# S5 mixer: the back rotation's two products go unsummed into the output products, the S5 matrices come on GpSimd's DMA queue, an input weight is split later

## The chip, the cores and the metric

The kernel runs on one core of a Trainium2 chip. The metric is the device time of one execution, in microseconds (us). Before the change it is 1264.65 us, the median of three runs (1264.57 to 1264.82). Five engines run their own instruction streams and meet at semaphores: TensorE (PE in the profile; its weight loads are PEld), VectorE (DVE), ScalarE (ACT), GpSimd (POOL) and SyncE (SP), which here only issues DMAs.

## The reference

The model is a trunk of four residual layers over 256 tokens of width 1024. The mixers are HGRN2, mLSTM, S5 and HGRN2 again, each followed by a SwiGLU layer. The change lies in the S5 mixer, a complex diagonal state space with 64 groups of 16 channels and 64 states each:

```python
def _s5_mixer(x, w_in, a_re, a_im, log_dt, b_re, b_im, c_re, c_im, d_skip, w_out):
    u = (x @ w_in)
    ...                      # abar, bbar from a, dt, b
    def step(carry, ub):
        bu_re = jnp.einsum('blgc,gpc->blgp', ub, bbar_re)
        bu_im = jnp.einsum('blgc,gpc->blgp', ub, bbar_im)
        pr, pi, sr, si = lax.associative_scan(_s5_combine, (a_r, a_i, bu_re, bu_im), axis=1)
        ...
        y = jnp.einsum('blgp,gcp->blgc', sr, c_re) - jnp.einsum('blgp,gcp->blgc', si, c_im)
    ...
    y = jax.nn.gelu(y + d_skip * u)
    za, zb = jnp.split(y @ w_out, 2, axis=-1)
    return za * jax.nn.sigmoid(zb)
```

## The kernel before

Large products are made of three: each fp32 weight is split into a high half (`hi`, a copy on ScalarE, line 129) and a low half (`lo`, a subtraction on VectorE, line 130), and `mm3` issues hi times hi, lo times hi and hi times lo. Weights arrive in units of 1 MB (tile `w`, line 108, issued by SP); `wstage` takes the next unit of a fixed plan and stages up to `ahead` units further.

The S5 stage works on four pairs of blocks, p = 0 to 3, each with 16 of the 64 groups; the 256 tokens are cut into 64 chunks of four, and the scans run over the chunks. For each pair `load_in` brings the input matrices (tiles `bm`, twice 512 KB) and the rotation tables (`cs`, 768 KB), `load_out` the output matrices (`ch`, 512 KB, and `cw`, twice 256 KB). Then:

- `inputs(p)` multiplies the transposed input projection `s5u` by `bm` on TensorE (line 1151).
- `forth(p)` rotates the result on VectorE (four products, one sum) and runs four scans (line 1167), so that a real scan does for the complex one.
- `back(p)` rotates back: two products (lines 1173 and 1174) and their sum (line 1176), which goes to `s5hs`.
- `outputs(p)` adds on TensorE, in two PSUM banks of the tag `t`, the products with `cw` (line 1190) and the C products of `ch` with `s5hs` (line 1197); ScalarE applies gelu into `ys`.
- `turn` transposes `ys` on TensorE (line 1207) into another `t` bank, copies the high half (ScalarE) and subtracts for the low half (VectorE, line 1212), into `xx`. The output products `a` (`out_piece`, weights `w_so`) of that pair start behind it, and the bank is free again.

`land` transposes the input projection into `s5u` on VectorE (line 1128); `project` makes that projection. `table_out` writes the tables `cs` to memory in an earlier step, during the layer before. The program is written as a list of such calls; a scheduler sets the order on each engine from it, by priorities and costs of its own, and puts in the waits. In `s5hs` the scanned states are shifted by one position, so that a C product takes the state ahead of its chunk; what happens inside a chunk comes from the `cw` products.

Of the kernel before, what the change touches and what calls it, by code (L numbers as in the profile page):

```python
# [9 lines left out]
F32 = mybir.dt.float32  # L10
# [4 lines left out]
ALU = mybir.AluOpType  # L15
AX = mybir.AxisListType

P = 128
# [16 lines left out]
class Trunk:  # L35
# [821 lines left out]
    def s5_prepare(self):  # L857


        nc, a = self.nc, self.a  # L860
# [4 lines left out]
        c = self.s5const  # L865
# [6 lines left out]
        tt, ts, stt = nc.vector.tensor_tensor, nc.vector.tensor_scalar, nc.vector.scalar_tensor_tensor  # L872
# [11 lines left out]
        def temps(*shape):  # L884
            n = int(np.prod(shape))
            dims = "abcd"[: len(shape)]
            out = []
            for tag, bufs in (("t0", 1), ("t1", 1)):
                t = tile_(tag, [P, 1024], bufs=bufs)[:, :n]
                kw = dict(zip(dims, shape))  # L890
                out.append(t.rearrange(f"p ({' '.join(dims)}) -> p {' '.join(dims)}", **kw))
            return out
# [84 lines left out]

        def table_out(b):
            cs, neg = k["cs"], temps(16, 64)[0]
            nc.scalar.mul(neg, cs[:, 1], -1.0)  # L980
            for i in range(2):
                for row, x in enumerate((cs[:, 0], neg, cs[:, 1])):
                    nc.sync.dma_start(self.s5_cs[2 * b + i][:, :, row].rearrange("p e (f c) -> p e f c", f=4),
                                      x[:, 8 * i : 8 * i + 8].rearrange("p (e f) c -> p e f c", e=2))
# [82 lines left out]
        for b in range(2):  # L1067
            spans[b] += [lambda b=b: table_start(b)] + [lambda n=n: table_double(n) for n in (1, 2, 4, 8, 16, 32)] + [lambda b=b: table_out(b)]
# [8 lines left out]
    def s5(self, gb):  # L1077
        nc, tc = self.nc, self.tc
        tt = nc.vector.tensor_tensor
# [15 lines left out]
        with tc.tile_pool(name=self.uid("s5"), bufs=1, reuse_waits="tile") as mp, \  # L1095
# [1 line left out]
            tl = lambda tag, shape, bufs=2: wp.tile(shape, F32, tag=tag, name=self.uid(tag), bufs=bufs)  # L1097
            u = mp.tile([P, 32, 64], F32, name="s5u")
            rr = [mp.tile([P, 2, 4, 64], F32, name=f"s5rr{i}") for i in range(2)]
            hs = [mp.tile([P, 2, 2, 4, 65], F32, name=f"s5hs{i}") for i in range(2)]  # L1100
            rot = [mp.tile([P, 2, 2, 256], F32, name=f"s5rot{i}") for i in range(3)]
            for r in rr:
                nc.gpsimd.memset(r[:, :, :, 0:1], 0.0)
            for h in hs:
                nc.gpsimd.memset(h[:, :, :, :, 0:1], 0.0)
            bm, cw, ch, tables, wi, pxs = {}, {}, {}, {}, {}, {}

            def load(dst, tag, src, i, bufs=2):
                dst[i] = tl(tag, list(src[i].shape), bufs)
                nc.sync.dma_start(dst[i], src[i])  # L1110

            def load_in(p):
                for b in (2 * p, 2 * p + 1):
                    load(bm, "bm", self.s5_b, b)
                load(tables, "cs", self.s5_cs, p)

            def load_out(p):
                load(ch, "ch", self.s5_ch, p)
                for b in (2 * p, 2 * p + 1):
                    load(cw, "cw", self.s5_cw, b, 4)  # L1120

            load_in(0)
            load_out(0)

# [4 lines left out]

            def project(n, h, tag, mid=None):  # L1130
                if n not in wi:
                    wi[n] = self.wstage("w_si", 2 * n) + self.wstage("w_si", 2 * n + 1, ahead=1 - n)
                ps = self.bank(tag)
                self.as_part({h: ps}, wi[n], mid=mid)
                return ps
# [17 lines left out]

            def forth(p):

                x, g, y = rot
                r, cs = rr[p % 2], tables[p]
                r4 = self.s5_r4[:, 8 * p : 8 * p + 8].rearrange("p (e f) -> p e f", e=2)
                nc.scalar.copy(r[:, :, :, 1:], r4[:, :, :, None].broadcast_to([P, 2, 4, 63]))
                for e in range(2):  # L1160
                    px = pxs.pop(2 * p + e).rearrange("p (r x) -> p r x", r=2)
                    tt(x[:, e], px, cs[:, e, 0:1].broadcast_to([P, 2, 256]), ALU.mult)
                    tt(y[:, e], px[:, ::-1], cs[:, e, 1:3], ALU.mult)
                tt(x, x, y, ALU.add)
                for e in range(2):
                    for i in range(2):
                        nc.vector.tensor_tensor_scan(g[:, e, i], r[:, e].rearrange("p f c -> p (f c)"), x[:, e, i], 0.0, ALU.mult, ALU.add)  # L1167

            def back(p):

                x, g, y = rot
                h, cs = hs[p % 2], tables[p]
                tt(x, g, cs[:, :, 0:1].broadcast_to([P, 2, 2, 256]), ALU.mult)
                tt(y, g[:, :, ::-1], cs[:, :, 2:0:-1], ALU.mult)
                many = lambda t: t.rearrange("p e r (f c) -> p (e r f) c", f=4)
                tt(h.rearrange("p e r f c -> p (e r f) c")[:, :, 1:], many(x), many(y), ALU.add)

            pieces, todo = [], []
            col = lambda f: slice(f * P, (f + 1) * P)
# [1 line left out]
            def outputs(p):  # L1181


                py, h = [self.bank("t") for _ in range(2)], hs[p % 2]
                at = lambda g, e, f: py[g][64 * e : 64 * e + 64, 64 * f : 64 * f + 64].rearrange("p (j c) -> p j c", j=4)
                for f in range(4):
                    for g in range(2):
                        for e in range(2):
                            w = cw[2 * p + e].rearrange("p (f j g c) -> p f j g c", f=4, j=4, g=2)
                            nc.tensor.matmul(at(g, e, f), u[:, 8 * p + 4 * e + f, :], w[:, f, :, g, :], start=f == 0, stop=False, skip_group_check=True)  # L1190
                for f in range(4):
                    for i in range(2):
                        for g in range(2):
                            for e in range(2):
                                r = slice(64 * g, 64 * g + 64)
                                c = ch[p].rearrange("p i j (f c) -> p i j f c", f=8)
                                nc.tensor.matmul(at(g, e, f), h[r, e, i, f, 0:64], c[r, i, :, 4 * e + f, :], start=False, stop=f == 3 and i == 1, skip_group_check=True)
                ys = tl("ys", [P, 4, P], 1)
                for g in range(2):
                    self.act(ys.rearrange("p j (f g c) -> p g f j c", f=4, g=2)[:, g], py[g][:, 0:256].rearrange("p (f j c) -> p f j c", f=4, j=4), AF.Gelu_apprx_tanh)  # L1200
                todo.append((ys, 2 * p))
# [13 lines left out]
            def few(n):  # L1215
                for _ in range(min(n, len(pieces))):
                    out_piece(0, *pieces.pop(0))

            land(project(0, 0, "g"), 0, 0)
            land(project_part(1, 0, "g"), 0, 1)  # L1220
            self.table("gelu_apprx_tanh_and_others")
            inputs(0)
            last = project_part(1, 1, "a")
            forth(0)
            land(last, 8, 1)
            load_in(1)
            more = project(1, 0, "a")
            back(0)
            inputs(1)
            outputs(0)  # L1230
            forth(1)
            load_out(1)
            land(more, 16, 0)
            more = project(1, 1, "a", lambda: turn(*todo.pop(0)))
            land(more, 16, 1)
            back(1)
            load_in(2)
            inputs(2)
            outputs(1)
            forth(2)  # L1240
            load_out(2)
            few(3)
            turn(*todo.pop(0))
            few(1)
            back(2)
            load_in(3)
            inputs(3)
            outputs(2)
            forth(3)
            load_out(3)  # L1250
# [194 lines left out]
```

## Time and profile before

| | us |
|---|---|
| median of three runs | 1264.65 |
| profiled execution, its time | 1264.65 |
| profiled execution, its span | 1262.9 |
| TensorE busy | 1241.5 |
| VectorE busy | 957.0 |
| ScalarE busy | 706.3 |
| GpSimd busy | 36.1 |

The S5 stage lies between about 641 and 736 us of the span. The granted TensorE clock is full there. In the profile's rows an instruction is named by line, engine, operation and tiles, the output ahead of the arrow; a bracket gives the idle time of the engine ahead of a row and what ended it. Small fp32 products appear as two records each.

### The profile page before, as it was taken

The numbers are of one execution on the slowest core, as the hardware profiler recorded it, in microseconds if no ns is written. First come the engines' busy times: TensorE is split into PE (matmuls) and PEld (weight loads), VectorE is DVE, ScalarE is ACT, GpSimd is POOL, SyncE is SP. The second block draws the span as 40 slices with busy tenths as digits, with TensorE's granted clock in tenths as the row PEclk, the third lists the DMA queues.
The fourth block names the chain that finished last, engine by engine and source line by source line (L and its number), as shares of the span: only waits on it lengthen the run. The fifth ranks groups of instructions, "written<-read, shape, count | busy, mean of one in ns | idle before, by whom it ended". The sixth has DMA issues, their size and how long they took to land. (4 is left out here: it accounts for less than half of the span.)

```text
span 1262.9 us, 21506 instructions
## 1 busy us (share of the span) xinstructions
PE 1241.5 (98%) x8541; PEld 1037.0 (82%) x8541; DVE 957.0 (76%) x1703; ACT 706.3 (56%) x1144; POOL 36.1 (3%) x58
## 2 busy tenths in 40 slices
PE   9999999999999999999998999999999999999997
PEld 7977888888798888888876678888879778888886
DVE  6887899876787799866599687666595887766664
ACT  7755576565467555666443455555458654555551
POOL 0000000000100100000000000000000000000000
PEclk9999999999999999999999999999999999999999
DMA  8733466765373266656569446555545432745530
GB/s 317 292 135 134 173 220 229 254 221 200 108 277 142 100 256 238 231 202 231 176 244 350 175 162 249 190 200 177 190 179 192 159 132 106 276 172 195 189 144 34
DMA packets 46340, 247.91 MB, mean 196 GB/s; under 512 B 5504, under 2 KB 11024, under 8 KB 19872
## 3 DMA queue, kind: packets, MB, share of 16 engines
q1 hardware_dynamic: 46112, 246.46, 53.4%
q8 instruction: 67, 1.10, 0.3%
q14 instruction: 33, 0.27, 0.1%
q0 software_dynamic: 128, 0.09, 0.0%
HBM read 233.94 MB, written 12.58 MB: 195 GB/s over the span
## 5 line engine op out<-in xcount | busy, mean ns | idle before, releaser
L130 DVE TENSOR_TENSOR lo<-w,hi 128x1024 fp32r<-128x1024 f32 x389 | 471.8, 1219 | 115.7 <-ACT hi L129 107.9
L129 ACT CAST hi<-w 128x1024 fp32r<-128x1024 f32 x389 | 407.2, 1051 | 198.8 <-PE a L160 118.1
L189 PE MATMUL g<-xx,hi 128*128 128x512 f32 x1024 | 358.2, 395 | 0.0
L192 PE MATMUL g<-xx,lo 128*128 128x256 f32 x1024 | 267.1, 281 | 0.0
L189 PEld LDWEIGHTS g<-xx,hi 128*128 128x128 f32 x1024 | 186.7, 188 | 34.6
L192 PEld LDWEIGHTS g<-xx,lo 128*128 128x128 f32 x1024 | 192.5, 188 | 10.3
L159 PE MATMUL g<-hi,xx 128*128 128x512 f32 (+1 forms) x416 | 167.7, 404 | 3.1 <-ACT xx L269 2.9
L161 PE MATMUL g<-lo,xx 128*128 128x512 f32 (+1 forms) x416 | 165.7, 400 | 0.1
L160 PE MATMUL g<-hi,xx 128*128 128x512 f32 (+1 forms) x416 | 164.7, 397 | 0.0
L160 PE MATMUL a<-hi,hl 128*128 128x512 f32 x344 | 135.4, 394 | 0.0
L159 PE MATMUL a<-hi,hh 128*128 128x512 f32 x344 | 135.4, 396 | 0.0
L161 PE MATMUL a<-lo,hh 128*128 128x512 f32 x344 | 135.4, 394 | 0.0
L329 ACT COPY sum<-g 128x256 f32<-128x256 f32 x128 | 47.7, 373 | 147.7 <-PE g L189 147.6
L330 DVE TENSOR_TENSOR sum<-g,sum 128x256 f32<-128x256 f32 x128 | 54.1, 423 | 69.4 <-ACT sum L329 68.8
L159 PEld LDWEIGHTS g<-hi,xx 128*128 128x128 f32 x416 | 78.4, 189 | 21.9 <-ACT xx L269 4.7
L161 PEld LDWEIGHTS g<-lo,xx 128*128 128x128 f32 x416 | 78.2, 188 | 18.4 <-DVE lo L130 1.5
L160 PEld LDWEIGHTS g<-hi,xx 128*128 128x128 f32 x416 | 78.5, 189 | 15.9
L161 PEld LDWEIGHTS a<-lo,hh 128*128 128x128 f32 x344 | 64.6, 188 | 15.0
L160 PEld LDWEIGHTS a<-hi,hl 128*128 128x128 f32 x344 | 64.5, 188 | 15.0 <-DVE hl L319 0.5
L159 PEld LDWEIGHTS a<-hi,hh 128*128 128x128 f32 x344 | 64.1, 188 | 13.5 <-ACT hh L318 0.6
L159 PE MATMUL g<-xx,hi 128*128 128x256 f32 x200 | 56.6, 283 | 0.0
L160 PE MATMUL g<-xx,lo 128*128 128x256 f32 x200 | 56.5, 283 | 0.0
(299 smaller groups left out, 1729.1 us busy)
## 6 DMA issues: line engine op xcount, KB each, us to landing
w<-in_w_gu SPq DMA_DIRECT2D x88, 1024.0 KB, 4.8
w<-in_w_dn SPq DMA_DIRECT2D x44, 1024.0 KB, 4.8
w<-in_w_hg SPq DMA_DIRECT2D x30, 1024.0 KB, 4.9
w<-in_w_ml SPq DMA_DIRECT2D x12, 1024.0 KB, 5.1
gb<-in_ln SPq DMA_DIRECT2D x8, 1024.0 KB, 4.6
w<-in_w_ho SPq DMA_DIRECT2D x8, 1024.0 KB, 4.9
w<-in_w_so SPq DMA_DIRECT2D x8, 1024.0 KB, 8.8
s5b<-st SPq DMA_DIRECT2D x16, 256.0 KB, 2.0
```

The lines of the kernel that those rows point to most:

```text
L129: self.nc.scalar.copy(hi, x)
L130: self.nc.vector.tensor_tensor(lo, x, hi.bitcast(F32), ALU.subtract)
L159: mm(ps, lh, rh, start=start, stop=False)
L160: mm(ps, ll, rh, start=False, stop=False)
L161: mm(ps, lh, rl, start=False, stop=stop)
L189: whole = lambda: mm(ps, hi[:, c], self.xx[:, k].rearrange("p i t -> p (i t)"), start=k == 0, stop=k == KD - 1)
L192: mm(ps[:, S:], lo[:, c], self.xh[:, k], start=False, stop=False)
L329: nc.scalar.copy(t, ps[:, S:])
L330: nc.vector.tensor_tensor(t, ps[:, 0:S], t, ALU.add)
```

## The change

`back` no longer sums. It writes its two products to two tiles, `hs[0]` and `hs[1]`, shifted by one element, and the C products run over both: 64 instead of 32 for a pair. For that, one column of the tables is set to zero when they are made. There were two `hs` tiles, one for each second pair; now the two belong to one pair, so that the next `back` waits for this pair's C products. Scratch tiles `rot` go from three to two. The loads of `bm`, `cs`, `ch` and `cw` are issued by GpSimd instead of SP, and `bm` has four buffers instead of two. In `project`, the second input weight unit no longer stages a third one with it.

```diff
@@ table_out
             cs, neg = k["cs"], temps(16, 64)[0]
+            nc.gpsimd.memset(cs[:, :, :, 63:64], 0.0)
@@ s5
-            hs = [mp.tile([P, 2, 2, 4, 65], F32, name=f"s5hs{i}") for i in range(2)]
-            rot = [mp.tile([P, 2, 2, 256], F32, name=f"s5rot{i}") for i in range(3)]
+            hs = [mp.tile([P, 1025], F32, name=f"s5hs{i}") for i in range(2)]
+            rot = [mp.tile([P, 2, 2, 256], F32, name=f"s5rot{i}") for i in range(2)]
...
-                nc.sync.dma_start(dst[i], src[i])
+                nc.gpsimd.dma_start(dst[i], src[i])
...
-                    load(bm, "bm", self.s5_b, b)
+                    load(bm, "bm", self.s5_b, b, 4)
@@ project
-                    wi[n] = self.wstage("w_si", 2 * n) + self.wstage("w_si", 2 * n + 1, ahead=1 - n)
+                    wi[n] = self.wstage("w_si", 2 * n) + self.wstage("w_si", 2 * n + 1, ahead=0)
@@ back
-                x, g, y = rot
-                h, cs = hs[p % 2], tables[p]
-                tt(x, g, cs[:, :, 0:1].broadcast_to([P, 2, 2, 256]), ALU.mult)
-                tt(y, g[:, :, ::-1], cs[:, :, 2:0:-1], ALU.mult)
-                many = lambda t: t.rearrange("p e r (f c) -> p (e r f) c", f=4)
-                tt(h.rearrange("p e r f c -> p (e r f) c")[:, :, 1:], many(x), many(y), ALU.add)
+                g, cs = rot[1], tables[p]
+                for h, src, w in zip(hs, (g, g[:, :, ::-1]), (cs[:, :, 0:1].broadcast_to([P, 2, 2, 256]), cs[:, :, 2:0:-1])):
+                    tt(h[:, 1:].rearrange("p (e r x) -> p e r x", e=2, r=2), src, w, ALU.mult)
@@ outputs
-                    for i in range(2):
+                    for i, h in ((0, hs[0]), (1, hs[0]), (0, hs[1]), (1, hs[1])):
...
-                                nc.tensor.matmul(at(g, e, f), h[r, e, i, f, 0:64], c[r, i, :, 4 * e + f, :], ...)
+                                x = 64 * (8 * e + 4 * i + f)
+                                nc.tensor.matmul(at(g, e, f), h[r, x : x + 64], c[r, i, :, 4 * e + f, :], ...)
```

The scheduler orders the changed program anew. (In these rows a scan is named by its general form, and numbers behind a name count the tiles.) On VectorE, around the second pair's back rotation and the first turn's subtraction (`xx` from `t1273`), before:

```order
L1167 SCALAR_TENSOR_TENSOR s5rot1_6918<-s5rr1_6914,s5rot0_6917 128x256 x4
L1212 TENSOR_TENSOR xx_83<-t1273_7304,xx_83 128x4x2x64
L1173 TENSOR_TENSOR s5rot0_6917<-s5rot1_6918,cs1257_7115 128x1024
L1128 STREAM_TRANSPOSE s5u_6912<-a1272_7291 128x16x32
L1174 TENSOR_TENSOR s5rot2_6919<-s5rot1_6918,cs1257_7115 128x1024
L130 TENSOR_TENSOR lo1301_7507<-w1299_7504,hi1300_7506 128x1024
L1176 TENSOR_TENSOR s5hs1_6916<-s5rot0_6917,s5rot2_6919 128x16x64
L130 TENSOR_TENSOR lo1303_7511<-w1299_7504,hi1302_7510 128x1024
```

and of the change:

```order
L1168 SCALAR_TENSOR_TENSOR s5rot1_6920<-s5rr1_6916,s5rot0_6919 128x256 x4
L1175 TENSOR_TENSOR s5hs0_6917<-s5rot1_6920,cs1252_7106 128x1024
L1175 TENSOR_TENSOR s5hs1_6918<-s5rot1_6920,cs1252_7106 128x1024
L130 TENSOR_TENSOR lo1301_7570<-w1299_7567,hi1300_7569 128x1024
L1212 TENSOR_TENSOR xx_83<-t1273_7336,xx_83 128x4x2x64
L130 TENSOR_TENSOR lo1303_7574<-w1299_7567,hi1302_7573 128x1024
L130 TENSOR_TENSOR lo1319_7807<-w1317_7804,hi1318_7806 128x1024
L1129 STREAM_TRANSPOSE s5u_6914<-a1272_7323 128x16x32
L130 TENSOR_TENSOR lo1321_7811<-w1317_7804,hi1320_7810 128x1024
```

The turn's subtraction stood ahead of the back rotation and now stands behind its two products and a split; the transposition into `s5u`, for which the third pair's `inputs` wait, stands behind the subtraction and two further splits. At the fourth pair and the third turn (`t1316`), VectorE before:

```order
L1167 SCALAR_TENSOR_TENSOR s5rot1_6918<-s5rr1_6914,s5rot0_6917 128x256 x4
L1212 TENSOR_TENSOR xx_83<-t1316_7695,xx_83 128x4x2x64
L1173 TENSOR_TENSOR s5rot0_6917<-s5rot1_6918,cs1307_7540 128x1024
L1174 TENSOR_TENSOR s5rot2_6919<-s5rot1_6918,cs1307_7540 128x1024
L130 TENSOR_TENSOR lo1334_7813<-w1332_7810,hi1333_7812 128x1024
L1176 TENSOR_TENSOR s5hs1_6916<-s5rot0_6917,s5rot2_6919 128x16x64
```

and of the change:

```order
L1168 SCALAR_TENSOR_TENSOR s5rot1_6920<-s5rr1_6916,s5rot0_6919 128x256 x4
L1175 TENSOR_TENSOR s5hs0_6917<-s5rot1_6920,cs1307_7602 128x1024
L1175 TENSOR_TENSOR s5hs1_6918<-s5rot1_6920,cs1307_7602 128x1024
L130 TENSOR_TENSOR lo1334_7938<-w1332_7935,hi1333_7937 128x1024
L1212 TENSOR_TENSOR xx_83<-t1316_7789,xx_83 128x4x2x64
```

Here too the subtraction went behind two products and a split. On TensorE the fourth pair's first eight cw products (16 records) stood ahead of the first output product that waits for that subtraction (line 160 into `a1285`, behind three that do not); now all its cw and C products stand behind such products. GpSimd's queue of the change, from the normalisation's power of the first half (`rs1223`) to the third pair's tables (`cs1276`) (a part is left out, with loads of the same kinds):

```order
L202 TENSOR_TENSOR rs1223_6840<-rs1223_6840,root_79 128x1
L1111 DMA bm1234_6925<-s5b0_1809 128x1024
L1111 DMA bm1235_6927<-s5b1_1810 128x1024
L1111 DMA cs1236_6929<-s5cs0_1833 128x1536
L202 TENSOR_TENSOR rs1229_6877<-rs1229_6877,root_79 128x1
L1111 DMA ch1237_6931<-s5ch0_1825 128x1024
...
L1111 DMA bm1274_7358<-s5b4_1813 128x1024
L1111 DMA bm1275_7360<-s5b5_1814 128x1024
L1111 DMA bm1305_7598<-s5b6_1815 128x1024
L1111 DMA bm1306_7600<-s5b7_1816 128x1024
L1111 DMA cs1276_7362<-s5cs2_1835 128x1536
```

Before, GpSimd had only the two powers and small clears here. The fourth pair's `bm` now stand ahead of the third pair's `cs`, and two `bm` and a `cs` ahead of the second power (`rs1229`).

More of the change, by code (lines that the diff above doesn't have):

```diff
@@ L1104, in s5 @@
             for h in hs:
-                nc.gpsimd.memset(h[:, :, :, :, 0:1], 0.0)
+                nc.gpsimd.memset(h[:, 0:1], 0.0)
             bm, cw, ch, tables, wi, pxs = {}, {}, {}, {}, {}, {}
@@ L1154, in forth @@
             def forth(p):
-                x, g, y = rot
+                x, g = rot
                 r, cs = rr[p % 2], tables[p]
@@ L1162, in forth @@
                     tt(x[:, e], px, cs[:, e, 0:1].broadcast_to([P, 2, 256]), ALU.mult)
-                    tt(y[:, e], px[:, ::-1], cs[:, e, 1:3], ALU.mult)
-                tt(x, x, y, ALU.add)
+                    tt(g[:, e], px[:, ::-1], cs[:, e, 1:3], ALU.mult)
+                tt(x, x, g, ALU.add)
                 for e in range(2):
@@ L1169, in back @@
             def back(p):
-                x, g, y = rot
-                h, cs = hs[p % 2], tables[p]
-                tt(x, g, cs[:, :, 0:1].broadcast_to([P, 2, 2, 256]), ALU.mult)
-                tt(y, g[:, :, ::-1], cs[:, :, 2:0:-1], ALU.mult)
-                many = lambda t: t.rearrange("p e r (f c) -> p (e r f) c", f=4)
-                tt(h.rearrange("p e r f c -> p (e r f) c")[:, :, 1:], many(x), many(y), ALU.add)
+                g, cs = rot[1], tables[p]
+                for h, src, w in zip(hs, (g, g[:, :, ::-1]), (cs[:, :, 0:1].broadcast_to([P, 2, 2, 256]), cs[:, :, 2:0:-1])):
+                    tt(h[:, 1:].rearrange("p (e r x) -> p e r x", e=2, r=2), src, w, ALU.mult)
             pieces, todo = [], []
@@ L1181, in outputs @@
             def outputs(p):
-                py, h = [self.bank("t") for _ in range(2)], hs[p % 2]
+                py = [self.bank("t") for _ in range(2)]
                 at = lambda g, e, f: py[g][64 * e : 64 * e + 64, 64 * f : 64 * f + 64].rearrange("p (j c) -> p j c", j=4)
@@ L1196, in outputs @@
                                 c = ch[p].rearrange("p i j (f c) -> p i j f c", f=8)
-                                nc.tensor.matmul(at(g, e, f), h[r, e, i, f, 0:64], c[r, i, :, 4 * e + f, :], start=False, stop=f == 3 and i == 1, skip_group_check=True)
+                                x = 64 * (8 * e + 4 * i + f)
+                                nc.tensor.matmul(at(g, e, f), h[r, x : x + 64], c[r, i, :, 4 * e + f, :], start=False, stop=f == 3 and i == 1 and h is hs[1], skip_group_check=True)
                 ys = tl("ys", [P, 4, P], 1)
```

## Prediction

> **What bounds the kernel now.** I read the page first, then the windows of the stage that the change touches, then the chain of waits there, then TensorE's and VectorE's timelines. On the page, TensorE is the busy engine and carries the largest share of the chain; the third row prices a weight's copy on ScalarE (busy us, mean ns):
>
> ```profile
> PE 1241.5 (98%) x8541; PEld 1037.0 (82%) x8541; DVE 957.0 (76%) x1703; ACT 706.3 (56%) x1144; POOL 36.1 (3%) x58
> PE 41%; DVE 3%; ACT 1%; issue 0%; DVEq 0%; POOL 0%; ACTq 0%; POOLq 0%
> L129 ACT CAST hi<-w 128x1024 fp32r<-128x1024 f32 x389 | 407.2, 1051 | 198.8 <-PE a L160 118.1
> ```
>
> That average hides the S5 stage. The table of windows (us; busy time with instruction counts of PE, PEld, DVE, ACT, POOL; granted clock; DMA share; GB/s) shows the opposite there:
>
> ```profile
> 657.00:668.00 11.00, 9.34 (x237) 7.79 (x227) 10.93 (x15) 0.71 (x2) 0.00 (x0) 1.00 0.87 320
> 668.00:683.00 15.00, 12.65 (x291) 10.13 (x288) 14.91 (x19) 8.28 (x10) 0.00 (x0) 1.00 0.81 304
> 683.00:697.00 14.00, 11.61 (x278) 9.43 (x282) 13.88 (x17) 3.76 (x5) 0.00 (x0) 1.00 0.97 384
> 697.00:711.00 14.00, 12.53 (x136) 9.30 (x131) 14.00 (x17) 4.91 (x6) 0.00 (x0) 1.00 0.44 171
> 711.00:736.00 25.00, 24.62 (x165) 19.39 (x162) 12.77 (x17) 10.67 (x13) 0.00 (x0) 1.00 0.36 126
> ```
>
> From 657 to 711 VectorE never rests and TensorE does; after 711 TensorE is full again. The DMA engines are 97% busy from 683 to 697. The chain of waits says the same in order of time (start, duration, what): VectorE up to the third turn's subtraction (L1212), then TensorE without a break to the last turn's transposes (L1207).
>
> ```profile
> 683.85 0.68 DVE s5rot L1162
> ...
> 704.87 0.96 DVE xx L1212
> ...
> 718.70 0.45 PE t L1207 x4
> ...
> 720.29 1.08 DVE xx L1212
> ```
>
> TensorE's timeline names each rest and its releaser in brackets (records here come in twos: 64 records of L1197 are the 32 products of a pair):
>
> ```profile
> 667.36 0.47 PE L1151 MATMUL g<-s5u,bm 128*32 128x64 f32 x17 [1.66 <-issue]
> 668.84 1.16 PE L1197 MATMUL t<-ch,s5hs 64*64 64x64 f32 x64
> 669.93 0.50 PE L159 MATMUL a<-hi,xx 128*128 128x512 f32 x1
> 670.27 0.39 PE L160 MATMUL a<-hi,xx 128*128 128x512 f32 x1
> 670.50 0.39 PE L161 MATMUL a<-lo,xx 128*128 128x512 f32 x1
> 677.73 1.03 PE L1190 MATMUL t<-cw,s5u 128*64 128x64 f32 x28 [1.24 <-DVE xx L1212]
> 679.48 1.99 PE L1151 MATMUL g<-s5u,bm 128*32 128x64 f32 x128 [0.29 <-DVE s5u L1128]
> 682.95 1.16 PE L1197 MATMUL t<-ch,s5hs 64*64 64x64 f32 x64 [0.82 <-DVE s5hs L1176]
> 693.08 1.03 PE L1190 MATMUL t<-cw,s5u 128*64 128x64 f32 x28 [1.26 <-DVE xx L1212]
> 696.60 1.16 PE L1197 MATMUL t<-ch,s5hs 64*64 64x64 f32 x64 [1.13 <-DVE s5hs L1176]
> 703.28 0.69 PE L1190 MATMUL t<-cw,s5u 128*64 128x64 f32 x16
> 705.87 0.50 PE L160 MATMUL a<-hi,xx 128*128 128x512 f32 x1 [1.48 <-DVE xx L1212]
> 718.54 0.60 PE L1207 MATMUL t<-ident,ys 128*128 128x128 f32 x4
> ```
>
> The rests sum to 1.66+1.24+0.29+0.82+1.26+1.13+1.48 = 7.9 us. Only about 2 us of it (0.82+1.13) waits for the sum that the change removes; 4.0 us (1.24+1.26+1.48) waits for the turn's subtraction.
>
> **The change, part by part.** VectorE's rows that price it (start, duration):
>
> ```profile
> 676.63 1.04 DVE L1212 TENSOR_TENSOR xx<-t,xx 128x512 fp32r<-128x512 f32 x1
> 678.71 0.71 DVE L1128 STREAM_TRANSPOSE s5u<-a 128x512 f32<-128x512 f32 x1
> 694.07 1.22 DVE L1174 TENSOR_TENSOR s5rot<-s5rot,cs 128x1024 f32<-128x1024 f32 x1
> 695.32 1.23 DVE L1176 TENSOR_TENSOR s5hs<-s5rot,s5rot 128x1024 f32<-128x1024 f32 x1
> 704.79 1.02 DVE L1212 TENSOR_TENSOR xx<-t,xx 128x512 fp32r<-128x512 f32 x1
> 708.00 1.22 DVE L130 TENSOR_TENSOR lo<-w,hi 128x1024 fp32r<-128x1024 f32 x1
> 709.13 1.22 DVE L1176 TENSOR_TENSOR s5hs<-s5rot,s5rot 128x1024 f32<-128x1024 f32 x1
> ```
>
> The sums go. A rotation product, a weight split and a sum each take 1.13 us start to start (708.00 to 709.13), so VectorE loses 4 x 1.13 = 4.5 us of work. That would be worth most of itself if what follows moved up with it.
>
> The turn's subtraction moves back. In the order it now stands behind the next pair's two products and a split, where it stood ahead of them. On the chain this subtraction releases TensorE, the sum does not. For the third turn (704.79), I count all VectorE work from the first pair's rotation: less three sums (-3.39), plus two products (+2.27), plus one split (+1.13): nothing is left of the saving. For the first turn it is one sum less: -1.13+2.27+1.13 = +2.3. Beside that come waits: with the output weights split earlier, the split ahead of the first rotation waits for its copy on ScalarE, between 0 and one copy (1.05 us, the page's third row); I take a third, 0.35. An instruction right behind its producer starts 1.25 us later (694.07 to 695.32), not 1.13; the addition and the scans now follow each other directly in three pairs: +0.35. One wait of the first subtraction for its own copy, and one of the third pair's first product for TensorE: 0 to 1, taken as 0.4 together. The third subtraction is then at about +1.1, and no gain.
>
> The third pair's inputs wait for the transposed input projection (L1128, 678.71). It now stands behind the first subtraction and two splits: the subtraction +2.9 from 676.63, then 0.94+1.13+1.13, which gives 682.7 instead of 678.7. TensorE's rest of 0.29 there grows to between 1 and 2; the 0.82 ahead of the second pair's C products goes in exchange.
>
> C products double. From 668.84 to 669.93 it is 1.09 us for a pair, 17 ns a record; four pairs cost 4 x 1.09 = 4.4 us of TensorE. The first three fill rests that open in front of them (after the three waits above, rests sum to about 8 us again, by this reckoning). The fourth pair's lie in the stretch from the third subtraction to the last transposes, which has no rest (705.87 to 718.54): +1.09 on the path. In that stretch also come the fourth pair's 16 first cw records (703.28 to 703.90, some 0.54 without the switch) and two large products (0.23 each, 670.27 to 670.50) that were done ahead of the wait and now stand behind it: +1.0. Fewer switches from small to large products (0.34 against 0.23) give back 0.2. The stretch grows by 1.9.
>
> [...]
>
> One set of hs instead of two: the next pair's products overwrite what the C products read. VectorE needs over 13 us from one back rotation to the next (695.32 to 709.13), TensorE under 3 us for the C products: no wait.
>
> The queue: twenty-four loads leave SP and stand on GpSimd's queue. The nearest rows are GpSimd's own earlier loads (ns), SP's issues, GpSimd's power, ScalarE's copies that wait for weights, and the cs loads' median time to landing:
>
> ```profile
> L682 POOL DMA_DIRECT2D taps<-in_ml_taps x1: 588/588/588, 330.0 to 330.0; - x1
> DMA to landing us min/median/max: 2.4/4.8/5.0
> 641.74 2.33 SPq L1110 DMA_DIRECT2D bm<-s5b  x2
> 644.12 0.43 SPq L1110 DMA_DIRECT2D cs<-s5cs  x1
> 647.27 0.72 POOL L202 TENSOR_TENSOR rs<-rs,root 128x1 f32<-128x1 f32 x1 [11.72 <-DVE rs L201]
> 680.39 2.00 ACT L129 CAST hi<-w 128x1024 fp32r<-128x1024 f32 x2 [3.03 <-DMA w<-in_w_so]
> 694.89 1.99 ACT L129 CAST hi<-w 128x1024 fp32r<-128x1024 f32 x2 [5.51 <-DMA w<-in_w_so]
> cs<-s5cs SPq DMA_DIRECT2D x4, 768.0 KB, 7.3
> ```
>
> An issue costs GpSimd 0.59 us against 0.43 on SP; GpSimd is idle, so that is covered. Two bm and a cs load now stand ahead of the normalisation's power (647.27); three issues from 641.74 at 0.59 each end by 643.5, or by 644.9 if the wait inside SP's 2.33 us for two repeats: covered by 2.4 us. SP, rid of them, can fetch output weights earlier; ScalarE's rests of 3.0 and 5.5 us go, but nothing on the chain waited for them. Four bm buffers let loads start earlier: bounds 0 to some us of collision, see below; I take 0, since every load has more lead than before. The later input split I put at 0: it is the same work, moved behind projections that keep TensorE full before 657 (the split's wait is counted above); if that cover fails, it is one split, 1.13. The zeroed column of cs is one GpSimd instruction in each of two earlier steps, on an engine 3% busy: 0.
>
> **Sum.** Third subtraction +1.1, stretch behind it +1.9, everything from the last transposes unchanged: +3.0. The profiled execution took 1264.65 us (span 1262.9 and 1.75 around it), which is the median of the runs: 1267.6. From 711 on TensorE is 98% busy, so a delay there is not regained.
>
> **Rivals.** Faster, the saving carries. If the third subtraction does not hold TensorE, because enough ready products stand ahead of it, doubled C products fill rests: 7.9 - 4.4 = 3.5 us less, 1261.1; with half of it 1262.9. For it: VectorE bounds 657 to 711 and loses 4.5 us. Against it: rests of 4.0 us belong to the subtraction, which moves back. It decides where the third subtraction ends before 704.
>
> A draw. If my waits on VectorE (1.1) do not come and the 16 cw records slip ahead, it is 1.09+0.46-0.2 = +1.3: 1266.0.
>
> Collision. The windows move 320, 304 and 384 GB/s; bringing weights (1.05 MB each, 2.7 us at 384 GB/s) and the fourth pair's bm ahead of the third pair's cs makes that cs late by one or two of them: +2.7 to +5.4 less cover; taken +3 on top: 1270.6. The same end is reached if each issue on GpSimd also waits for an instruction of VectorE, 1.2 us: that cs is the 17th load of the queue, 641.7 + 17 x (0.59+1.2) + 7.3 = 679.4, and it is needed at about 684, so it decides from (684-7.3-641.7)/17 = 2.1 us an issue on. For the collision: 97% DMA share. Against: 0.81 to 0.87 before 683 leaves room.
>
> [...]
>
> **Chances.** Forecast 0.42, collision 0.13, draw 0.27, faster 0.18. About 0.2% (2.5 us) is what a measurement of this kernel can tell from no change. The forecast's 1267.6 is just above it; with a fifth of its cases below it (0.08): slower 0.34+0.13 = 0.47, same 0.27+0.08 = 0.35, faster 0.18. Its own range is 1266.2 to 1269.0; the range of all runs from half of the faster case, 1262.5, to past the collision, 1271.5.
>
> **What would show it.** Right: the first and the third subtraction at about 679.5 and 705.9 instead of 676.63 and 704.79; the last transposes near 721.5; C products 2.2 us a pair; a rest of 1 to 2 us ahead of the third pair's inputs. Wrong: a third subtraction before 704.8, ScalarE or TensorE waiting for cs, ch, cw or bm, GpSimd's issues over 1.5 us, or C products far from 17 ns a record.

## The result, and the profile after

The changed kernel takes 1270.59 us (median of six runs, 1270.08 to 1272.16), the kernel before 1264.6 us on the same chip: a ratio of 1.0048 (95% interval 1.0038 to 1.0058). It is slower by some 6 us, where the forecast said 3. The profiled execution took 1270.08 us with a span of 1268.3 us, 5.4 us more than before, and is the one that the lines below come from.

The page of the changed kernel: busy times, the chain's shares by engine, and the DMA queue that it names instruction (packets, MB, share).

```profile
PE 1246.1 (98%) x8797; PEld 1042.4 (82%) x8797; DVE 953.4 (75%) x1699; ACT 705.7 (56%) x1144; POOL 49.8 (4%) x84
...
q8 instruction: 69, 1.13, 0.3%
...
PE 92%; DVE 4%; ACT 2%; issue 1%; DMA 0%; DVEq 0%; POOL 0%; ACTq 0%; POOLq 0%
```

TensorE is busy 4.6 us longer and has 256 records more, the doubled C products; VectorE has 3.6 us less to do. The last line has TensorE on 92% of the chain. The 41% of before is no measure to set against it: there the chain could be followed back only to 683.05 us, so that all its shares sum to 45% of the span. The row of the instruction queue (q8) is used further down; the page of before has for it:

```profile
q8 instruction: 67, 1.10, 0.3%
```

The windows of the S5 stage (columns as before: PE, PEld, DVE, ACT, POOL with counts, granted clock, DMA share, GB/s), changed kernel:

```profile
657.00:668.00 11.00, 9.57 (x200) 7.65 (x188) 11.00 (x16) 2.61 (x3) 1.50 (x3) 1.00 1.01 413
668.00:683.00 15.00, 11.19 (x193) 9.30 (x192) 12.46 (x16) 5.35 (x8) 3.19 (x6) 0.89 0.99 394
683.00:697.00 14.00, 12.85 (x380) 10.61 (x384) 13.71 (x17) 4.64 (x6) 1.61 (x3) 1.00 0.61 236
697.00:711.00 14.00, 12.38 (x275) 10.24 (x264) 13.54 (x16) 3.89 (x6) 0.00 (x0) 1.00 0.22 77
```

The second row is the one that stands out: TensorE does 1.46 us less there than before and has a clock of 0.89, and VectorE, which never rested here before, rests 2.5 us. The third row is better filled than before (12.85 against 11.61 us), the fourth is not (12.38 against 12.53). DMA traffic has moved forward: its share is about 1.0 up to 683 and falls behind it. TensorE's timeline names the rests:

```profile
661.44 0.51 PE L161 MATMUL a<-lo,xx 128*128 128x512 f32 x1 [0.98 <-issue]
...
667.58 0.47 PE L1152 MATMUL g<-s5u,bm 128*32 128x64 f32 x17 [0.45 <-issue]
667.98 1.15 PE L1189 MATMUL t<-cw,s5u 128*64 128x64 f32 x32
669.06 1.39 PE L1197 MATMUL t<-ch,s5hs 64*64 64x64 f32 x78
674.26 1.75 PE L1197 MATMUL t<-ch,s5hs 64*64 64x64 f32 x50 [3.81 <-issue]
...
679.56 0.60 PE L1207 MATMUL t<-ident,ys 128*128 128x128 f32 x4
...
685.70 2.31 PE L1152 MATMUL g<-s5u,bm 128*32 128x64 f32 x128 [1.05 <-DVE s5u L1129]
...
700.87 0.92 PE L1197 MATMUL t<-ch,s5hs 64*64 64x64 f32 x45 [0.26 <-issue]
...
709.65 0.50 PE L160 MATMUL a<-hi,xx 128*128 128x512 f32 x1 [1.36 <-DVE xx L1212]
...
712.42 1.15 PE L1189 MATMUL t<-cw,s5u 128*64 128x64 f32 x32
713.50 2.09 PE L1197 MATMUL t<-ch,s5hs 64*64 64x64 f32 x128
...
724.00 0.60 PE L1207 MATMUL t<-ident,ys 128*128 128x128 f32 x4
```

TensorE stops for 3.81 us in the middle of the first pair's C products, after 78 of 128 records. Their operands are there, no semaphore is named: the profile calls it "issue". Right behind that rest, the granted clock was 0.51 for 3.4 us, as three narrower windows show (same columns):

```profile
668.00:674.20 6.20, 2.45 (x112) 2.24 (x110) 6.17 (x9) 0.00 (x0) 2.13 (x4) 0.99 1.02 408
674.20:677.60 3.40, 3.34 (x54) 2.93 (x55) 3.30 (x5) 1.16 (x3) 0.53 (x1) 0.51 1.03 417
677.60:683.00 5.40, 5.40 (x28) 4.13 (x28) 3.00 (x4) 4.19 (x5) 0.53 (x1) 1.00 0.92 364
```

The chain of waits passes through that rest and goes on over ScalarE to VectorE (start, duration, what):

```profile
669.13 1.32 PE t L1197 x78
670.45 3.81 issue
674.26 1.75 PE t L1197 x50
...
680.54 1.10 ACT xx L91
...
684.94 0.72 DVE s5u L1129
...
708.54 1.07 DVE xx L1212
```

VectorE's own rows say the same from the other side. The first turn's subtraction waited 1.17 us for a copy that came out of the late transposes:

```profile
681.66 1.10 DVE L1212 TENSOR_TENSOR xx<-t,xx 128x512 fp32r<-128x512 f32 x1 [1.17 <-ACT xx L91]
...
684.94 0.71 DVE L1129 STREAM_TRANSPOSE s5u<-a 128x512 f32<-128x512 f32 x1
...
708.54 1.06 DVE L1212 TENSOR_TENSOR xx<-t,xx 128x512 fp32r<-128x512 f32 x1
```

With these starts and those of before, the stage falls into four legs that add up (us):

| leg, ending with | before | after | longer by | by the prediction |
|---|---|---|---|---|
| first turn's transposes (L1207) | 672.83 | 679.56 | +6.73 | |
| third pair's transposition into s5u | 678.71 | 684.94 | -0.50 | +4.0 with the leg above |
| third turn's subtraction (L1212) | 704.79 | 708.54 | -2.48 | -2.9 |
| last transposes (L1207) | 718.54 | 724.00 | +1.71 | +1.9 |
| sum | | | +5.46 | +3.0 |

The first leg alone is longer by more than the whole loss. The first two legs together are longer by 6.2 us where the prediction had 4.0, which is 2.2 of the 2.5 us by which it fell short. The first leg's loss lies on TensorE: the first pair's doubled C products +1.09, rests without a releaser 0.98 + 0.45 + 3.81 in place of 1.66, which is +3.58, and the halved clock an estimated +1.7 (half of 3.4). That is 6.4 of 6.7 us.

### The profile page after: what moved, and what is told of

It is laid out like the page before. It is cut to its first block, busy times and chain, and to the rows that moved or that the text cites. A ratio compares the mean times of both kernels' runs of the same rounds, so it can differ in the third digit from the quotient of the medians.

```text
span 1268.3 us, 22043 instructions
## 1 busy us (share of the span) xinstructions
PE 1246.1 (98%) x8797; PEld 1042.4 (82%) x8797; DVE 953.4 (75%) x1699; ACT 705.7 (56%) x1144; POOL 49.8 (4%) x84
## 4 chain that ended last, share of the span: by engine, by line
PE 92%; DVE 4%; ACT 2%; issue 1%; DMA 0%; DVEq 0%; POOL 0%; ACTq 0%; POOLq 0%
PE g L189 19%; PE g L159 10%; PE g L161 10%; PE g L160 10%; PE g L192 10%; PE a L159 9%; PE a L160 9%; PE a L161 9%; PE t L250 1%; DVE lo L130 1%; PE a L635 1%; PE t L1042 1%; PE a L515 1%; ACT L84 1%; PE t L423 0%
## 5 line engine op out<-in xcount | busy, mean ns | idle before, releaser
L192 PEld LDWEIGHTS g<-xx,lo 128*128 128x128 f32 x1024 | 192.4, 188 | 10.3
```

Of the source, the lines that this page charges most:

```text
L192: mm(ps[:, S:], lo[:, c], self.xh[:, k], start=False, stop=False)
```

## The experiments

Open was why TensorE rests without a releaser, and what the three edits of the change have to do with it: the doubled number of small products, the traffic of loads that come earlier, GpSimd's queue, or after all VectorE's order. In the table, "rests" is the sum of TensorE's rests put down to issue from 655 to 735 us, and "half clock" an estimate of the time lost to it, from the granted clock between 655 and 741 us (86 times one less the clock, which is given to two digits, so that it holds to within 0.4).

| kernel | median us | ratio to before, 95% | rests | half clock |
|---|---|---|---|---|
| before | 1264.3 to 1265.0 | | 1.7 | 0 |
| the change | 1270.59 | 1.0048 (1.0038 to 1.0058) | 5.5 | 1.7 |
| unsummed_only | 1274.60 | 1.0074 (1.0061 to 1.0087) | 9.7 | 3.4 |
| queue_split | 1266.03 | 1.0007 (0.9998 to 1.0015) | 2.5 | 0 |
| after_bm2 | 1278.62 | 1.0104 (1.0088 to 1.0119) | 8.0 | 5.2 |
| after_sync4 | 1273.93 | 1.0073 (1.0060 to 1.0085) | 8.6 | 3.4 |
| after_half | 1267.07 | 1.0019 (1.0010 to 1.0028) | 3.8 | 3.4 |
| after_so_small | 1269.03 | 1.0034 (1.0021 to 1.0046) | 3.1 | 3.4 |
| unsummed_so_small | 1267.91 | 1.0026 (1.0017 to 1.0036) | 4.8 | 1.7 |
| before_so_small | 1265.07 | 1.0000 (0.9991 to 1.0009) | 0.9 | 3.4 |
| after_turn_ahead | 1270.71 | 1.0050 (1.0038 to 1.0063) | 7.7 | 1.7 |
| after_spread | 1270.77 | 1.0041 (1.0027 to 1.0054) | 6.5 | 1.7 |
| sum_on_pool | 1271.12 | 1.0047 (1.0034 to 1.0059) | 1.1 | 3.4 |
| lo_on_pool | 1276.49 | 1.0097 (1.0083 to 1.0111) | 3.3 | 8.6 |

### The products alone: unsummed_only

The kernel before, with only the edit of back, outputs and the tables' zero column; loads on SP, two bm buffers and the early input split stay.

```diff
-                tt(h.rearrange("p e r f c -> p (e r f) c")[:, :, 1:], many(x), many(y), ALU.add)
+                for h, src, w in zip(hs, (g, g[:, :, ::-1]), (...)):
+                    tt(h[:, 1:].rearrange("p (e r x) -> p e r x", e=2, r=2), src, w, ALU.mult)
...
-                    for i in range(2):
+                    for i, h in ((0, hs[0]), (1, hs[0]), (0, hs[1]), (1, hs[1])):
```

> The kernel before with the unsummed products alone (back, outputs, the two tiles hs); loads on SP with two bm buffers and the input split as before. In the changed kernel's trace TensorE rests 3.81 us in the middle of the first pair's C products with no releaser (before: 1.66 us in that region), and its granted clock is halved for 3.4 us behind that. Theory F (fetch): TensorE's own instructions come by DMA, and the early loads, which keep the DMA engines at 99 to 101% from 657 to 683 us, make them late; so here, with the old loads, that rest stays near 1.7 us, and only the order costs, by the reckoning of the prediction +3.0 to +3.7: 1267.6 to 1268.3. Theory N (number): the doubled small products use up instructions faster than they come, whatever the loads; the rest is 3 to 4 us here too: about 1270.5.

It took 1274.60 us, 0.74% over before, and more than the whole change. TensorE's rests in its timeline:

```profile
666.70 0.47 PE L1152 MATMUL g<-s5u,bm 128*32 128x64 f32 x17 [1.06 <-issue]
...
672.01 1.02 PE L1197 MATMUL t<-ch,s5hs 64*64 64x64 f32 x50 [2.44 <-issue]
...
686.63 2.55 PE L1197 MATMUL t<-ch,s5hs 64*64 64x64 f32 x111 [2.47 <-issue]
...
700.43 0.42 PE L1152 MATMUL g<-s5u,bm 128*32 128x64 f32 x12 [2.41 <-issue]
...
706.17 0.92 PE L1197 MATMUL t<-ch,s5hs 64*64 64x64 f32 x45 [1.31 <-issue]
```

That is also 4 us more than either expectation allowed, since there are five rests and not one. The unsummed products alone bring the rests (9.7 us); the edits of queue, buffers and split do not have to be there for them, and together recover some 3 us (0.26%). The first two stops fall at the same records as in the changed kernel (17 from the end of one block's inputs, 50 from the end of the C products), with 17 + 32 + 78 = 127 records from the one to the other.

### The loads and the split alone: queue_split

```diff
-                nc.sync.dma_start(dst[i], src[i])
+                nc.gpsimd.dma_start(dst[i], src[i])
...
-                    load(bm, "bm", self.s5_b, b)
+                    load(bm, "bm", self.s5_b, b, 4)
...
-  self.wstage("w_si", 2 * n + 1, ahead=1 - n)
+  self.wstage("w_si", 2 * n + 1, ahead=0)
```

> The kernel before with the other edits alone: loads on GpSimd's queue, four bm buffers, the later input split; the sums stay. Theory F: the rest of TensorE without releaser grows to 3 us or more as in the changed kernel, with a dip of the clock, though there are no more small products than before: about 1267 to 1269. Theory N: the rest stays at 1.7 us, and time at 1264.6 to 1266 (one us for the order).

1266.03 us, 1.0007 with 1 inside the interval: no cost that can be told. The DMA engines were as full as in the changed kernel (windows):

```profile
657.00:668.00 11.00, 9.48 (x214) 7.68 (x216) 10.04 (x15) 3.56 (x4) 1.07 (x2) 1.00 1.01 419
668.00:683.00 15.00, 13.30 (x338) 10.60 (x330) 14.87 (x19) 6.06 (x8) 4.26 (x8) 1.00 0.94 376
```

With 1.01 and 0.94 of the DMA engines busy, the rests came to 2.5 us and the clock stayed full. Full DMA engines alone did not make the long rests here. One rest goes with these edits: that in the projection behind the first pair's inputs (1.52 us here, ending at 663.36, 0.98 us in the changed kernel) is there in every kernel with the later input split and in none with the earlier one.

### Which of the loads' edits matters: after_bm2 and after_sync4

The changed kernel with two bm buffers again, and the changed kernel with its loads on SP.

```diff
-                    load(bm, "bm", self.s5_b, b, 4)
+                    load(bm, "bm", self.s5_b, b)
```
```diff
-                nc.gpsimd.dma_start(dst[i], src[i])
+                nc.sync.dma_start(dst[i], src[i])
```

> The changed kernel with two bm buffers as before, so that bm loads start later; the queue is GpSimd's. Theory F: the DMA engines are less full before 683 us, the rest is between 1.7 and 3 us: 1268 to 1269.5. Theory N: as the changed kernel, 1270.6, rest near 3.8 us. If GpSimd's queue itself is the cause (its descriptors late), loads land late and engines wait for them by name: bm, cs, ch or cw as releasers.

> The changed kernel with its loads on SP, four bm buffers kept. If GpSimd's queue is the cause of the extra loss, it goes: about 1267.5. Theory F, where only the early start counts: DMA share near 100% before 683 us again and a rest of 3 us or more: about 1270. Theory N: rest of 3 to 4 us too: about 1270; the first kernel of this call parts F from N.

Two buffers cost 8 us against the change (1278.62): now bm came late, as one row of TensorE's timeline shows.

```profile
669.39 3.21 PE L1152 MATMUL g<-s5u,bm 128*32 128x64 f32 x111 [4.09 <-DMA bm<-s5b]
```

The loads on SP cost 3 us (1273.93), as much as the products alone. Both times lie beyond what was expected (1270.6 at most). So GpSimd's queue is no burden with four buffers: it helps. With two, the kernel is slower than the products alone, from which it differs in the queue and in the later split. Why the rests are shorter with four buffers on GpSimd than with four on SP (5.5 against 8.6 us) I could not settle; the DMA share of the second window is higher on GpSimd (0.99 against 0.86), so it is not the share.

### Half of the C products: after_half

The C products of the second tile are left out (256 records), as many as before remain; VectorE's order is that of the change.

```diff
-                    for i, h in ((0, hs[0]), (1, hs[0]), (0, hs[1]), (1, hs[1])):
+                    for i, h in ((0, hs[0]), (1, hs[0])):
```

> The changed kernel without the C products of the second tile hs[1]: half of the output's state term is left out, and TensorE has 256 records of C products again; loads and VectorE's work stay. Theory so far: TensorE's instructions come in blocks of 16 KB by DMA, 256 instructions or 128 small records each; a block of small products lasts 2.2 us and the next one is there only every 5 to 6.5 us while loads run, so TensorE stops at block ends. Then its rests without releaser fall from 5.5 to some 2.5 us (as with the loads moved alone), the clock dip goes, and time is about 1266 (order and queue +1). If the rests come from something else in the change, 4 to 5.5 us of them stay and time is above 1268.

1267.07 us, 3.5 less than the change. No rest falls into the C products any more, and the third subtraction starts at 705.66, 0.87 later than before: that is the shift by VectorE's order that the prediction worked out as 1.1, here by itself, as VectorE has no rest in this kernel from 657 us to that subtraction. What remains over before is not that shift alone, since behind a rest of 3.16 us for this subtraction the granted clock was 0.55 from 706.7 to 713.6 us (3.4 us lost by the estimate in the table):

```profile
706.76 0.79 PE L160 MATMUL a<-hi,xx 128*128 128x512 f32 x1 [3.16 <-DVE xx L1212]
```

### Less data traffic: after_so_small, unsummed_so_small, before_so_small

In three kernels each load of an output weight brings 64 KB instead of 1 MB and the splits read these few columns repeated, so that the output weights are not the real ones; the number and kind of instructions on the engines stay.

```diff
-        nc.sync.dma_start(st[:, 0:w], src)
+        few = 128 if name == "w_so" else w
+        nc.sync.dma_start(st[:, 0:few], src[:, 0:few])
...
+                self.halve(st[:, None, 0:few].broadcast_to([P, 1024 // few, few]), wide(hi), wide(lo))
```

> The changed kernel with 64 KB instead of 1 MB brought for each output weight unit w_so; ScalarE's and VectorE's splits read those 128 columns eight times over, so only DMA traffic falls, by 7.5 MB, and the output products use wrong weights. Theory D (data traffic delays the instruction blocks): rests of TensorE without releaser fall from 5.5 to 1.5 us or less, no clock dip, 1264.5 to 1266. Theory X (a block's time is fixed, whatever the traffic): rests stay at 4 to 5.5 us, 1269 to 1270.5.

> The same cut of the output weights' traffic in the kernel with the unsummed products alone (1274.6, rests of 9.7 us without releaser, two clock dips). Theory D: rests under 3 us and no dips, about 1266.5 to 1268. Theory X: rests of 8 us or more, about 1273.

> The kernel before with 64 KB instead of 1 MB for each output weight unit (the output products use wrong weights; splits keep their work). It tells what the data traffic costs the kernel before: if TensorE's 1.66 us rest there is a late instruction block made late by traffic, it falls below 1 us; time falls by no more than 1 us all the same, since VectorE carries the chain there: 1263.5 to 1264.6. If traffic held more, the time falls by over 2 us.

The rests became shorter in each: 5.5 to 3.1, 9.7 to 4.8, 1.7 to 0.9 us. The products alone gained 6.7 us by it (1274.60 to 1267.91), the changed kernel 1.6, the kernel before nothing (ratio 1.0000): with small weights it lost 3.4 us to the half clock, which it did not with the full ones. So in these kernels more traffic went with longer rests, but with a DMA share of 0.66 (668 to 683 us) and 0.49 (683 to 697) the products alone still rested 4.8 us. Traffic is a factor here, not the source.

### VectorE's order undone: after_turn_ahead

The changed kernel, with each back rotation's products ordered behind the turn's subtraction, as before the change.

```diff
+                    i = tt(h[:, 1:]..., src, w, ALU.mult).ins
+                    if p:
+                        tc.add_manual_dep(i, self.turned.name, dep, reason="turn ahead of back")
...
-                tt(ol, src, oh.bitcast(F32), ALU.subtract)
+                self.turned = tt(ol, src, oh.bitcast(F32), ALU.subtract).ins
```

> The changed kernel with a dependency that orders each back rotation behind the turn called before it, so that the turn's subtraction stands ahead of the two products again, as before the change. Theory O (order costs about 3 of the 6 us, rests the other 3): third subtraction near 706 instead of 708.5, time 1267 to 1268. If the late instruction blocks alone cost the 6 us and the order nothing, it stays at 1270 to 1271.

1270.71 us: nothing gained. VectorE's rows of the second and third subtraction show why:

```profile
696.34 1.18 DVE L1215 TENSOR_TENSOR xx<-t,xx 128x512 fp32r<-128x512 f32 x1 [0.89 <-ACT xx L91]
...
709.11 1.09 DVE L1215 TENSOR_TENSOR xx<-t,xx 128x512 fp32r<-128x512 f32 x1 [0.87 <-ACT xx L91]
```

They now wait for their operand, and the first starts at 681.78 (681.66 in the change). In the changed kernel VectorE's order is not what delays the turns; TensorE's late transposes are. The rests grew from 5.5 to 7.7 us in this kernel, so that up to some 2 us that the order may have gained could be hidden; the theory that the loss is mainly VectorE's order fell here.

### Large products between the small ones: after_spread

The first pair's outputs are put into the middle of a projection, so that large products lie between its inputs and its C products.

```diff
-            outputs(0)
...
-            more = project(1, 1, "a", lambda: turn(*todo.pop(0)))
+            more = project(1, 1, "a", lambda: outputs(0))
+            turn(*todo.pop(0))
```

> The changed kernel with the first pair's outputs called in the middle of the second input projection, so that twelve large products (2.8 us) stand on TensorE between the second pair's input products and the first pair's cw and C products; loads, counts and VectorE's instructions are the same. Theory of late instruction blocks: a run of small products is cut in two, the 3.81 us rest in the first pair shrinks by about 2.8 to near 1 us and the clock dip behind it goes; time falls by 1.5 to 4: 1266.5 to 1269. If the rest has another cause, tied to the C products themselves (their tiles, their number in one group), it stays at 3 to 4 us and time at 1270 or above, the outputs being later.

```profile
674.73 1.16 PE L1197 MATMUL t<-ch,s5hs 64*64 64x64 f32 x62 [0.43 <-issue]
...
688.20 3.54 PE L1197 MATMUL t<-ch,s5hs 64*64 64x64 f32 x112 [3.71 <-issue]
```

The rest of 3.81 us shrank to 0.43, as it should if the next instructions come at a time of their own and large products fill the time until then. But the second pair's C products then stopped for 3.71 us, in a window (683 to 697 us) with a granted clock of 0.88, and the time is 1270.77 us. The local cure worked and the loss moved on.

### The sum elsewhere: sum_on_pool and lo_on_pool

If the number of small products is the trouble, VectorE can be relieved without it: the kernel before with back's sum on GpSimd, and the kernel before with every second low half of the output weights on GpSimd.

```diff
-                tt(h..., many(x), many(y), ALU.add)
+                nc.gpsimd.tensor_tensor(h..., many(x), many(y), ALU.add)
```
```diff
-                self.halve(part, hi, lo)
+                self.halve(part, hi, lo, nc.gpsimd if name == "w_so" and i else nc.vector)
```

> The kernel before with the back rotation's sum on GpSimd instead of VectorE: VectorE loses the same 4.5 us as in the change, and TensorE gets no further small products. No row prices a sum of this size on GpSimd (a clear of 2048 took it 1.81 us, so half of that, 0.9, is a lower bound). If the loss in the change came from TensorE's doubled C products, this version does not lose: 1262.5 to 1265. If GpSimd takes over 3 us for a sum or holds VectorE up, C products come late and it is 1266 or more.

> The kernel before with the low half of every second output weight part (eight of sixteen w_so splits) made on GpSimd instead of VectorE: VectorE loses 8 x 1.13 = 9.0 us, twice what the change took from it, GpSimd gets eight instructions of 2.3 to 3.3 us (as its sums took in the run before), and TensorE no further small products. If VectorE's work alone held the stage, the turns' subtractions come some 2 to 5 us earlier and time falls to 1261 to 1263. If the stage is held by TensorE's late instruction blocks and by waits for the slower splits, it gains nothing or loses: 1264.5 to 1268, with lo from GpSimd as TensorE's releaser.

Both are slower than before, 0.47% and 0.97%. On GpSimd the sum took (ns, min, median, max):

```profile
L1176 POOL TENSOR_TENSOR s5hs<-s5rot,s5rot x4: 2337/2786/3260, 666.6 to 711.8; 128x1024 f32<-128x1024 f32 x4
```

against 1.22 us on VectorE, and TensorE waited for it four times, 6.4 us in all. With the splits on GpSimd, VectorE's row of one rotation shows the other cost:

```profile
706.44 1.19 DVE L130 TENSOR_TENSOR lo<-w,hi 128x1024 fp32r<-128x1024 f32 x1
707.56 3.35 DVE L1173 TENSOR_TENSOR s5rot<-s5rot,cs 128x1024 f32<-128x1024 f32 x1
710.84 1.21 DVE L1174 TENSOR_TENSOR s5rot<-s5rot,cs 128x1024 f32<-128x1024 f32 x1
```

The middle one takes 3.35 us instead of 1.22. It starts while GpSimd runs this split, which ends at 709.83:

```profile
706.59 3.24 POOL L130 TENSOR_TENSOR lo<-w,hi 128x1024 fp32r<-128x1024 f32 x1 [1.20 <-ACT hi L129]
```

So here VectorE's product took 2.1 us longer beside GpSimd's split. The time lies 8 us beyond the slower expectation: the third turn's subtraction came so late that TensorE stood still for it, and 8.6 us went to the half clock.

```profile
714.20 0.80 PE L160 MATMUL a<-hi,xx 128*128 128x512 f32 x1 [7.80 <-DVE xx L1212]
```

No version tried beats the kernel before.

## Why the prediction was right in direction and short in size

The forecast was 1267.6 us with 1266.2 to 1269.0 as its own range; the measured 1270.59 lies above that range and inside the one over all cases (1262.5 to 1271.5). That it came within 3 us is in part luck. The forecast put queue, buffers and split at 0 and the products with VectorE's order at +3.0. Measured alone, products and order cost 9.6 us (unsummed_only), and the other edits won some 3 us of it back.

- **The C products.** Right: 2.09 us for the 128 records of the last pair, where 2.2 was said, and 16 to 17 ns a record.
- **The stretch behind the third subtraction.** +1.71 for a predicted +1.9. All cw products and two large products stand behind the wait, as worked out.
- **VectorE's order.** The count of sums, products and splits held: from the transposition into s5u to the third subtraction VectorE gained 2.48 us (predicted 2.9), and in after_half, where TensorE does not hold it up, the third subtraction is 0.87 us late for a predicted 1.1.
- **The third subtraction at 705.9.** This is the term that was mis-sized: +1.1 predicted, +3.75 measured. The first subtraction shows it already (679.5 predicted, 681.66 measured), and the last transposes inherit it (721.5 and 724.00). The step that failed is the first leg, up to 682.7 for the transposition (684.94 measured). It was put together from VectorE's instructions and waits alone. TensorE arrived later still, with 3.6 us more of rest and an estimated 1.7 us lost to the half clock.
- **"Rests sum to about 8 us again".** They did: 0.98 + 0.45 + 3.81 + 1.05 + 0.26 + 1.36 = 7.9. But only 2.4 of it waits for VectorE, and 5.5 for nothing that the profile names (each of these rests ended behind a packet of the instruction queue, as is shown below). The sum was right and its make-up wrong. The trace of before showed the first of these rests (1.66, at the same 17 records); the prediction quoted that row, added it up and then gave it no mechanism that the doubled products could act on.
- **The third pair's inputs.** A rest of 1.05 us, predicted 1 to 2. The wait for the sum ahead of the C products is gone, and VectorE never waited for C products to free `hs`.
- **The queue, at nothing.** Nothing by itself (queue_split), but not beside the doubled products, where the three edits together saved some 3 us. No cost came of it either: GpSimd's issues, once begun, took 0.53 us, and its power started at 646.84 (647.27 before), as its rows show. The loads landed later (bm 10.3 us at the median, cs 8.8), but no computing instruction waited for one. GpSimd alone did, for 2.0, 2.5 and 0.4 us, ahead of further loads.

```profile
643.31 0.53 POOL L1111 DMA_DIRECT2D bm<-s5b  x1 [5.84 <-DVE x L225]
643.84 0.53 POOL L1111 DMA_DIRECT2D cs<-s5cs  x1
646.84 0.73 POOL L202 TENSOR_TENSOR rs<-rs,root 128x1 f32<-128x1 f32 x1 [2.47 <-DVE rs L201]
```

- **The rivals.** The measured time lies beside the collision's 1270.6, but that is chance: no tables came late and no issue grew long beside VectorE's work. The saving did not carry, because the first leg held what VectorE saved. With VectorE 100% busy from 657 to 668 in sums, products and scans, GpSimd's three issues there took 0.53 us each. The later landings have full DMA engines (1.01) beside them.

**What the rests are.** The experiments show that they come with the number of small products, fall at the same records in several kernels, shrink with less traffic and shrink where large products lie ahead. The pages add a count, for the queue that they name instruction: TensorE's 8541 records (each with its weight load) on 67 packets of the instruction queue before, and 8797 on 69 after, are 127.5 records a packet both times, and 256 more records brought two more packets. That is the distance between the two stops. 128 large products last 128 x 0.23 = 29 us, 128 small ones 128 x 0.017 = 2.2 us.

The trace sets the rests beside these packets. It holds every DMA packet by itself, those of the instruction queue (all 67 of before and all 69 of the change with 16384 bytes) too. Beside the rests (in us; the last column counts the records of TensorE up to its stop):

| kernel | packet starts | has landed | TensorE goes on | later by | records so far |
|---|---|---|---|---|---|
| before | 664.97 | 665.87 | 667.36 | 1.5 | 4412 |
| the change | 659.11 | 660.14 | 661.44 | 1.3 | 4285 |
| the change | 665.12 | 666.19 | 667.58 | 1.4 | 4412 |
| the change | 671.71 | 672.82 | 674.26 | 1.4 | 4539 |
| the change | 698.39 | 699.50 | 700.87 | 1.4 | 5176 |
| unsummed_only | 669.49 | 670.53 | 672.01 | 1.5 | 4539 |

The fourteen kernels have 46 rests put down to issue between 655 and 735 us. 45 of them end 1.2 to 1.6 us after such a packet has landed, and at one of seven places that lie 127 or 128 records apart, or twice that (records so far: 4285, 4412, 4539, 4793 or 4794, 4921, 5049, 5175 to 5177). The 46th (0.54 us, in queue_split) fits neither. That TensorE stops because its next 127 or 128 records have not come is the author's reading; no row names it.

The interval was measured in part. Behind each of the 45 resumptions the next packet started 1.0 to 4.3 us later (3.7, 4.1, 3.8 and 2.4 us in the changed kernel) and took 0.9 to 1.1 us, and the rests ended 1.2 to 1.6 us after their packets. 128 small products, 2.2 us, are done sooner than that. What holds the packet's start back stays open, and no run changed the instruction packets without changing the products.

## What to carry to other kernels

Here, trading four sums for 256 more records of small products cost 9.6 us (unsummed_only), where the products' own time is an estimated 4.4 us (256 x 17 ns). Before such a trade, look in the timeline for rests put down to issue within runs of small products, check whether they recur after a fixed number of records (127 to 128 here), and set them beside the packets of the instruction queue in the trace. Such rests were no constant here: they came to 1.7 us before and to 9.7 us with the doubled products alone. When a wait is predicted for one engine, work out the arrival of the other side too, since the later one sets the time.

## What the runs showed of the hardware

- TensorE rested up to 3.8 us inside products whose operands were there, and went on 1.2 to 1.6 us after a 16 KB packet of the instruction queue had landed (above). None of the prediction's terms allowed for it.
- The granted clock fell to about half behind some rests and not behind others. Behind the rest of 3.81 us in the change it was 0.51 from 674.2 to 677.6, and behind that of 3.16 us in after_half 0.55 from 706.7 to 713.6. In after_sync4, with a rest of 1.85 us ending at 662.01, it was 0.84 from 657 to 668. In before_so_small it was 0.67 behind a rest of 2.27 us ending at 678.91:

```profile
672.00:678.90 6.90, 4.64 (x32) 3.46 (x31) 6.90 (x10) 4.27 (x6) 0.00 (x0) 1.00 0.45 168
678.90:682.30 3.40, 3.39 (x130) 3.32 (x134) 3.40 (x4) 0.59 (x1) 0.00 (x0) 0.67 0.30 87
```

  and in unsummed_only it was 1.00 behind a rest of 2.44 us ending at 672.01 (in both windows from 672.0 to 683.0). So the length of a rest did not tell by itself. Twelve of the fourteen kernels had a clock below 1.00 between 655 and 741 us (table); what decides it was not shown.
- GpSimd's sums and splits of 128x1024 took 2.3 to 3.4 us. In lo_on_pool three VectorE instructions of 128x1024 that ran beside such a split (a split, a sum and a product) took 2.91, 2.77 and 3.35 us, against 1.2 for most of their kind; the 3.35 us begin inside GpSimd's split and end 1.1 us behind it. Why they took longer was not shown.
